# A hybrid HGRN2 and attention block: the second pair's accumulators evicted earlier in program order, the norm weight's row on GpSimd's queue

## The chip, the cores and the metric

The kernel runs on one core of one Trainium2 chip. The metric is the device time of one execution in microseconds (us); the time given for a kernel is the median of its runs. A profile is one further execution, recorded by the hardware.

The engines: PE (TensorE, matmuls; PEld are its weight loads), DVE (VectorE, elementwise), ACT (ScalarE, activations and copies), POOL (GpSimd) and SP (SyncE, which here only issues DMAs). Each works through its own queue in order. SPq, ACTq and POOLq are the DMAs that an engine issues.

## What is computed

One layer of a block with 256 rows of 2048 channels: an RMS norm, one wide input projection, an HGRN2 recurrence and a chunked attention on parts of it, a gated merge, an output projection, and an MLP with a squared ReLU. Cut to the part that the change lies in:

```python
u = rms_norm(h, norm_mix_w)
z = u @ w_in                                   # 2048 x 11264
hq, hf, hi, hg, aq, ak, av, gates = jnp.split(z, SPLIT_POINTS, axis=-1)
f = jax.nn.sigmoid(hf)
g = lb + (1.0 - lb) * f
log_g, kk = jnp.log(g), 1.0 - g
q = jax.nn.silu(hq) * (HG_DK ** -0.5)
o = hgrn2_scan(heads(q), heads(kk), heads(hi), heads(log_g))   # 8 heads of 128
y_a = rms_norm(o, hg_norm_w) * jax.nn.silu(hg)
y_b = chunk_band_attention(aq, ak, av, rel_bias)
merged = gate_a * (y_a @ w_branch_a) + gate_b * (y_b @ w_branch_b)
h = h + merged @ w_out
h = h + jnp.square(jax.nn.relu(rms_norm(h, norm_mlp_w) @ w_up)) @ w_down
out = rms_norm(h, norm_final_w)
```

## The kernel before

**Precision and matmuls.** Every large product is made of three: weights and activations are split into a high and a low part (`split`, L86: a cast on ACT to `wh`, L87, and a subtraction on DVE to `wl`, L88), and high x high, high x low and low x high are added up in one accumulator in PSUM. `weights` (L107) loads the weights by SP's queue, 1 MB at a time (L124), into three buffers `raw`, and splits each half into `wh` and `wl`, of which there are four buffers each.

**Accumulators.** `new_acc` (L146) takes one of two buffers (`ps_acc`). `gemm` (L149) makes a product with tokens on the partitions, `gemm_t` (L173, with `mm_t`, L180: matmuls at L185, L186 and L189) one with channels on the partitions. In the second form the two halves of an accumulator are added at the end by `add_parts` (L191): a copy on ACT (L193), then an addition on DVE (L194). Only after the addition is the buffer free for the accumulator after the next.

**The start.** The first loop (L219) makes hf and hq of pair 0 side by side while their inputs arrive. A pair is two of the eight HGRN2 heads: 256 channels of hf and 256 of hq. Then come, in program order, the constants (L248 to L285: lower bounds, masks, the row `hgw` of the norm weight spread over all partitions, L283), the eviction of pair 0 (L288 to L290: `f0`, `z0`), the product hf of pair 1 (`acc_f1`, L291), and the row norms: `squares` (L212) loads the rows of x by SP's queue, squares them on ACT, and `rows` (L236) turns 1/rms into a row over all partitions (`rstd_t`).

**The first half of the heads.** For g = 0 the loop at L485 calls `fq(0)` and `fq(1)`. `fq` (L474) evicts hf and hq of its pair, if need be makes them first, and calls `hf_pair` (L307: multiply by rstd, sigmoid, bounds, logarithm, scan) and `hq_pair` (L325: multiply by rstd, sigmoid, product). In `fq(1)` the product hf is there already (`acc_f1`), hq is made at L478. Then follow `v_chunk` (L338, the product hi, matmuls at L157 to L159), `hgrn_scores` of pair 0 (L359), `hg_chunk` (L347, the product hg, which reads `hgw` at L355), the scores of pair 1, and their values.

`hgrn_scores` makes the scores of a pair in eight small products `ps` (L366, L406) and a last one (L432), with two PSUM buffers (tag `sm`); DVE takes each out with a multiplication (L367) and masked copies (L368, L413) into `sd`. What it needs of ACT and DVE beforehand is exponentials and products (`el`, `er`, `rr`, `kl`, `qr`, L377 to L399).

**What sets the order.** Each engine's queue is written by a scheduler, which goes by the program's order and by priorities: `add_parts` and `split` stand in a `high_priority` block, so they are put ahead of elementwise work, but only as far as the place of their call lets them. Sigmoid, logarithm and exponential are different tables of ACT; a change of table is an instruction of its own (ACT_TABLE_LOAD).

Of the kernel before, what the change touches and what calls it, by code (L numbers as in the profile page):

```python
# [16 lines left out]
P = 128  # L17
T = 256
NM = T // P
D = 2048  # L20
KD = D // P
# [5 lines left out]
DK = 128  # L27
# [5 lines left out]
C_HQ, C_HF, C_AQ, C_AK, C_GA, C_GB = 0, HG, 2 * HG, 3 * HG, 4 * HG, 4 * HG + D  # L33
# [17 lines left out]
def tile_hybrid_block(  # L51
# [5 lines left out]
    nc = tc.nc  # L57
# [38 lines left out]
    def new_act(what):  # L96

        return apool.tile([P, 4, 2, T], F32R, name=f"act_{what}", tag="act")
# [47 lines left out]
    def new_acc(what):  # L146
        return ps_acc.tile([P, 2, NC], F32, name=f"acc_{what}", tag="acc")
# [25 lines left out]
    def gemm_t(rhs, w, n0, nkt, what):  # L173

        acc = new_acc(what)
        for a in weights(w, n0, nkt, T, what):
            mm_t(acc, rhs, nkt, *a)
        return acc

    def mm_t(acc, rhs, nkt, kt, wh, wl):  # L180
        r = rhs[kt // 4][:, kt % 4]
        for cb in range(2):
            c = slice(cb * P, (cb + 1) * P)
            if kt:
                nc.tensor.matmul(acc[:, cb, 0:T], wl[:, c], r[:, 0, :], start=False, stop=False)  # L185
            nc.tensor.matmul(acc[:, cb, :], wh[:, c], r.rearrange("p u t -> p (u t)"),  # L186
                             start=kt == 0, stop=kt == nkt - 1)
            if kt == 0:
                nc.tensor.matmul(acc[:, cb, 0:T], wl[:, c], r[:, 0, :], start=False, stop=False)  # L189

    def add_parts(dst, acc):  # L191
        with tc.high_priority(offset=2000):
            nc.scalar.copy(dst, acc[:, :, T:])  # L193
            nc.vector.tensor_tensor(dst, acc[:, :, 0:T], dst, op=ALU.add)  # L194
# [5 lines left out]
    def h2(what, bufs=10):  # L200
        return hp.tile([P, 2, T], F32, name=what, tag="h2", bufs=bufs)

    xT = [new_act(f"x{c}") for c in range(4)]
# [76 lines left out]
    nc.gpsimd.memset(reset, 1.0)  # L280
    nc.gpsimd.memset(reset.rearrange("p (c t) -> p c t", t=CH)[:, :, 0:1], 0.0)
    hgw = const.tile([P, DK], F32, name="hgw")
    nc.sync.dma_start(hgw, bass.AP(tensor=hg_norm_w.tensor, offset=hg_norm_w.offset, ap=[[0, P], [1, DK]]))  # L283
    c128 = const.tile([P, 2, 4], F32, name="c128")
    nc.gpsimd.memset(c128, 1.0)  # L285

# [1 line left out]
    f0, z0 = h2("f0"), h2("zq0")  # L288
    add_parts(f0, accs[0])
    add_parts(z0, accs[1])  # L290
    acc_f1 = gemm_t(xT, w_in_t, C_HF + T, KD, "hf1")  # L291
# [4 lines left out]
    rstd_t = rows(rstd, "rstd")  # L296
    rstd8_t = const.tile([P, T], F32, name="rstd8_t")
    nc.vector.tensor_scalar(rstd8_t, rstd_t, 0.125, None, op0=ALU.mult)


    def z_t(col, what, dst, factor, acc=None):
# [5 lines left out]
    def hf_pair(u, f):  # L307

        nc.vector.tensor_tensor(f, f, bc(rstd_t, 1, 2), op=ALU.mult)
        nc.scalar.activation(f, f, AF.Sigmoid)  # L310
        for h in range(2):
            hh = 2 * u + h
            nc.vector.tensor_scalar(f[:, h, :], f[:, h, :], omlb[:, hh:hh + 1], lb[:, hh:hh + 1],
                                    op0=ALU.mult, op1=ALU.add)
        kk = h2(f"kk{u}")
        nc.vector.tensor_scalar(kk, f, -1.0, 1.0, op0=ALU.mult, op1=ALU.add)
        nc.vector.tensor_scalar(f, f, LN_MIN, None, op0=ALU.max)
        lg = h2(f"lg{u}")
        nc.scalar.activation(lg, f, AF.Ln)
        b = h2(f"b{u}")  # L320
        nc.vector.tensor_tensor_scan(b.rearrange("p h t -> p (h t)"), reset,
                                     lg.rearrange("p h t -> p (h t)"), 0.0, ALU.mult, ALU.add)
        return f, kk, b

    def hq_pair(u, z, g):  # L325

        nc.vector.tensor_tensor(z, z, bc(rstd_t, 1, 2), op=ALU.mult)
        s = h2(f"sq{u}")
        nc.scalar.activation(s, z, AF.Sigmoid)
        q = hp.tile([P, 2, NM, 192], F32, name=f"q{u}", tag="q", bufs=2)  # L330
        half = lambda a: a.rearrange("p h (m t) -> p h m t", t=P)
        nc.vector.scalar_tensor_tensor(q[:, :, :, 0:P], half(z), DK ** -0.5, half(s), op0=ALU.mult, op1=ALU.mult)
        odd = lambda a: a.rearrange("p h m (j u) -> p h m j u", u=2)[:, :, :, :, 1]
        for h in range(2):
            nc.vector.tensor_tensor(q[:, h, :, P:], odd(q[:, :, :, 0:P])[:, h], odd(half(g))[:, h], op=ALU.mult)
        return q
# [135 lines left out]
        return finish  # L472

    def fq(u):  # L474
        if u:
            f, z = h2(f"f{u}"), h2(f"zq{u}")
            add_parts(f, acc_f1 if u == 1 else gemm_t(xT, w_in_t, C_HF + u * T, KD, f"hf{u}"))
            add_parts(z, gemm_t(xT, w_in_t, C_HQ + u * T, KD, f"hq{u}"))  # L478
        else:
            f, z = f0, z0  # L480
        g, kk, b = hf_pair(u, f)
        return kk, b, hq_pair(u, z, g)

    out0 = out1 = None
    for g in range(2):  # L485
        ya.append(new_act(f"ya{g}"))
        u = 2 * g
        a0 = fq(u)
        if out1:
            out1()  # L490
        a1 = fq(u + 1)
        vs = v_chunk(g)
        s0 = hgrn_scores(u, *a0)
        gws = hg_chunk(g)
        s1 = hgrn_scores(u + 1, *a1)
        out0 = hgrn_out(g, 0, s0, vs, gws)

        def out1(g=g, s1=s1, vs=vs, gws=gws, out0=out0):
            finish = hgrn_out(g, 2, s1, vs, gws)
            out0()  # L500
            finish()
# [152 lines left out]
    for qd in range(NQ):  # L654
# [12 lines left out]
        for n in range(4):  # L667
            end = last and n == 3
            acc = gemm(uT, w_down, n * NC, KD, f"dn{qd}{n}", tail=8 if end else 0, kt0=qd * KD)
            for m in range(NM):  # L670
# [11 lines left out]
                f = rstd3[:, m:m + 1]  # L682
# [53 lines left out]
```

## Time and profile before

| | |
|---|---|
| median of 3 runs | 1480.14 us (1478.12 to 1481.28) |
| the profiled execution | 1478.41 us, its span in the trace 1476.7 us |
| mean granted clock of PE | 0.995 |
| matmuls of the products hf, `acc_hf` L186, 128x512 | 128, 416 ns each as recorded |
| matmuls of the MLP, `acc_up` L186, 128x512 | 1024, 398 ns each as recorded |
| `hgw`, SP's issue and its landing | issued at 19.54 us, landing 7.0 us later |
| `gw` with `hgw` (L355) | first at 120.0 us, 4 times, median 675 ns |
| GpSimd's idle time before the row norm's power (L94) | 29.84 us, to 39.76 us |
| PE by stretches of 20 us, 0 to 80 us: granted clock | 1.00, 0.91, 1.00, 0.83 |

How to read the profile: a line of a timeline is a start, a duration, the engine, the line of the kernel, the operation, and what it writes and reads; in square brackets stands how long the engine was idle before it and what ended that. Matmuls are pipelined, so a recorded duration is longer than the distance to the next start. A clock of 1.00 is the full rate of TensorE. The chain is followed back from the last instruction to what released it.

### The profile page before, as it was taken

Reading aid. Unit: us, or ns where it says so; the run is one execution under the profiler, and the core shown is the slowest. Engines: PE = TensorE matmul, PEld = TensorE weight load, DVE = VectorE, ACT = ScalarE, POOL = GpSimd, SP = SyncE. Lnnn points to the kernel's source line nnn. Section 1 sums busy time; section 2 is a strip of 40 time slices with the busy share of each in tenths; the row PEclk is TensorE's granted clock in tenths of the full one; section 3 lists DMA queues with packets and bytes.
Section 4 is the critical chain, followed back from the end, with each engine's and each line's share of the span. In section 5 each row is a group of like instructions: output and inputs, shape, how many; then the busy total and the mean of one; then the engine's idle time right before and its main releaser. Section 6 shows DMA issues by size and latency. Waiting matters only on the chain.

```text
span 1476.7 us, 18045 instructions
## 1 busy us (share of the span) xinstructions
PE 1452.6 (98%) x7244; PEld 1222.5 (83%) x7244; DVE 881.1 (60%) x1180; ACT 713.2 (48%) x894; POOL 28.8 (2%) x85
## 2 busy tenths in 40 slices
PE   8899999999999999999999999999999999999997
PEld 7788888888788888888888888888888888888886
DVE  6797987565644444666565554566545665556554
ACT  6764844464544444344445544455434553355443
POOL 2000001010000000000000000000000000000000
PEclk9899999999999999999999999999999999999999
DMA  8444444545455555557545555555555555555552
GB/s 305 181 164 150 152 171 145 189 126 195 137 171 199 197 187 188 198 177 279 176 175 192 198 184 190 198 174 197 199 190 183 198 176 194 200 175 196 194 188 102
DMA packets 49045, 272.85 MB, mean 185 GB/s; under 512 B 5056, under 2 KB 5952, under 8 KB 23488
## 3 DMA queue, kind: packets, MB, share of 16 engines
q1 hardware_dynamic: 45744, 264.85, 51.5%
q10 hardware_dynamic: 2448, 4.74, 0.9%
q0 software_dynamic: 768, 2.10, 0.7%
q8 instruction: 57, 0.93, 0.2%
q14 instruction: 28, 0.23, 0.0%
HBM read 269.57 MB, written 2.10 MB: 184 GB/s over the span
## 4 chain that ended last, share of the span: by engine, by line
PE 93%; DVE 3%; DMA 1%; issue 1%; ACT 1%; POOL 0%; SPq 0%; POOLq 0%; ACTq 0%
PE acc_up L186 16%; PE acc_dn L157 8%; PE acc_dn L159 8%; PE acc_dn L158 8%; PE acc_up L185 8%; PE acc_ak L186 2%; PE acc_wo L158 2%; PE acc_wo L159 2%; PE acc_gb L159 2%; PE acc_gb L158 2%; PE acc_wo L157 2%; PE acc_gb L157 2%; PE acc_ga L159 2%; PE acc_ga L158 2%; PE acc_ga L157 2%; PE acc_aq L186 2%
## 5 line engine op out<-in xcount | busy, mean ns | idle before, releaser
L186 PE MATMUL acc_up<-act_h,wh_up 128*128 128x512 f32 x1024 | 359.2, 398 | 0.0
L185 PE MATMUL acc_up<-act_h,wl_up 128*128 128x256 f32 x960 | 269.7, 281 | 0.0
L88 DVE TENSOR_TENSOR wl_dn<-raw_dn,wh_dn 128x1024 fp32r<-128x1024 f32 x128 | 156.7, 1224 | 149.6 <-ACT wh_dn L87 149.6
L186 PEld LDWEIGHTS acc_up<-act_h,wh_up 128*128 128x128 f32 x1024 | 190.6, 188 | 44.4
L87 ACT CAST wh_dn<-raw_dn 128x1024 fp32r<-128x1024 f32 x128 | 135.1, 1055 | 186.3 <-PE acc_dn L159 172.2
L88 DVE TENSOR_TENSOR wl_up<-raw_up,wh_up 128x1024 fp32r<-128x1024 f32 x128 | 156.6, 1224 | 106.0 <-ACT wh_up L87 105.8
L158 PE MATMUL acc_dn<-wl_dn,act_u 128*128 128x512 f32 x512 | 199.2, 389 | 0.0
L159 PE MATMUL acc_dn<-wh_dn,act_u 128*128 128x512 f32 x512 | 199.2, 389 | 0.0
L157 PE MATMUL acc_dn<-wh_dn,act_u 128*128 128x512 f32 x512 | 199.1, 389 | 0.0
L87 ACT CAST wh_up<-raw_up 128x1024 fp32r<-128x1024 f32 x128 | 134.7, 1052 | 121.1 <-PE acc_up L186 93.0
L185 PEld LDWEIGHTS acc_up<-act_h,wl_up 128*128 128x128 f32 x960 | 181.3, 189 | 1.4
L159 PEld LDWEIGHTS acc_dn<-wh_dn,act_u 128*128 128x128 f32 x512 | 96.1, 188 | 20.1
L157 PEld LDWEIGHTS acc_dn<-wh_dn,act_u 128*128 128x128 f32 x512 | 96.1, 188 | 19.9 <-DVE h L672 0.2
L158 PEld LDWEIGHTS acc_dn<-wl_dn,act_u 128*128 128x128 f32 x512 | 96.1, 188 | 19.9
L88 DVE TENSOR_TENSOR wl_gb<-raw_gb,wh_gb 128x1024 fp32r<-128x1024 f32 x32 | 39.2, 1225 | 47.8 <-ACT wh_gb L87 47.8
L88 DVE TENSOR_TENSOR wl_ga<-raw_ga,wh_ga 128x1024 fp32r<-128x1024 f32 x32 | 39.2, 1225 | 43.4 <-ACT wh_ga L87 43.4
L88 DVE TENSOR_TENSOR wl_wo<-raw_wo,wh_wo 128x1024 fp32r<-128x1024 f32 x32 | 39.2, 1224 | 35.6 <-ACT wh_wo L87 35.6
L87 ACT CAST wh_wo<-raw_wo 128x1024 fp32r<-128x1024 f32 x32 | 33.8, 1055 | 49.3 <-PE acc_wo L159 38.3
L87 ACT CAST wh_gb<-raw_gb 128x1024 fp32r<-128x1024 f32 x32 | 33.8, 1057 | 48.6 <-PE acc_gb L159 41.9
L87 ACT CAST wh_ga<-raw_ga 128x1024 fp32r<-128x1024 f32 x32 | 33.8, 1055 | 45.3 <-PE acc_ga L159 38.6
L186 PE MATMUL acc_hf<-act_x,wh_hf 128*128 128x512 f32 x128 | 48.9, 416 | 2.7 <-DVE f L194 2.7
L159 PE MATMUL acc_ga<-wh_ga,act_x 128*128 128x512 f32 x128 | 50.5, 394 | 0.0
(305 smaller groups left out, 2752.4 us busy)
## 6 DMA issues: line engine op xcount, KB each, us to landing
raw_up<-in_w_up_dram SPq DMA_DIRECT2D x64, 1024.0 KB, 4.9
raw_dn<-in_w_down_dram SPq DMA_DIRECT2D x64, 1024.0 KB, 4.9
raw_ga<-in_w_in_t_dram SPq DMA_DIRECT2D x16, 1024.0 KB, 5.0
raw_gb<-in_w_in_t_dram SPq DMA_DIRECT2D x16, 1024.0 KB, 5.0
raw_wo<-in_w_out_dram SPq DMA_DIRECT2D x16, 1024.0 KB, 4.9
raw_hi<-in_w_in_n_dram SPq DMA_DIRECT2D x8, 1024.0 KB, 4.9
raw_hg<-in_w_in_n_dram SPq DMA_DIRECT2D x8, 1024.0 KB, 4.9
raw_aq<-in_w_in_t_dram SPq DMA_DIRECT2D x8, 1024.0 KB, 4.8
```

Of the source, the lines that this page charges most:

```text
L87: (copy or nc.scalar.copy)(hi, src)
L88: nc.vector.tensor_tensor(lo, src, hi.bitcast(F32), op=ALU.subtract)
L157: nc.tensor.matmul(part(m), h, wh, start=kt == 0, stop=False)
L158: nc.tensor.matmul(part(m), h, wl, start=False, stop=False)
L159: nc.tensor.matmul(part(m), lo, wh, start=False, stop=kt == nkt - 1)
L185: nc.tensor.matmul(acc[:, cb, 0:T], wl[:, c], r[:, 0, :], start=False, stop=False)
L186: nc.tensor.matmul(acc[:, cb, :], wh[:, c], r.rearrange("p u t -> p (u t)"), start=kt == 0, stop=kt == nkt - 1)
```

## The change

Two edits. `hgw` is loaded by GpSimd's queue. And the eviction of pair 1 (the copy and addition of hf, the product hq with its copy and addition) is written ahead of the definitions and calls of the elementwise work, right behind the row norms; `fq` then takes the evicted tiles for pairs 0 and 1.

```diff
     hgw = const.tile([P, DK], F32, name="hgw")
-    nc.sync.dma_start(hgw, bass.AP(tensor=hg_norm_w.tensor, offset=hg_norm_w.offset, ap=[[0, P], [1, DK]]))
+    nc.gpsimd.dma_start(hgw, bass.AP(tensor=hg_norm_w.tensor, offset=hg_norm_w.offset, ap=[[0, P], [1, DK]]))
...
     rstd8_t = const.tile([P, T], F32, name="rstd8_t")
     nc.vector.tensor_scalar(rstd8_t, rstd_t, 0.125, None, op0=ALU.mult)
+
+    f1, z1 = h2("f1"), h2("zq1")
+    add_parts(f1, acc_f1)
+    add_parts(z1, gemm_t(xT, w_in_t, C_HQ + T, KD, "hq1"))
...
     def fq(u):
-        if u:
+        if u == 0:
+            f, z = f0, z0
+        elif u == 1:
+            f, z = f1, z1
+        else:
             f, z = h2(f"f{u}"), h2(f"zq{u}")
-            add_parts(f, acc_f1 if u == 1 else gemm_t(xT, w_in_t, C_HF + u * T, KD, f"hf{u}"))
+            add_parts(f, gemm_t(xT, w_in_t, C_HF + u * T, KD, f"hf{u}"))
             add_parts(z, gemm_t(xT, w_in_t, C_HQ + u * T, KD, f"hq{u}"))
-        else:
-            f, z = f0, z0
         g, kk, b = hf_pair(u, f)
         return kk, b, hq_pair(u, z, g)
```

Lines of the kernel from L299 on move down by 4, those behind `fq` by 6 (L366 becomes L370, L406 becomes L410). The products, their sizes and their order on PE up to the scores are the same.

## The prediction

> **What bounds the kernel now.** I read the page first, then the waits of the first 300 us, then the timelines of PE, ACT and DVE around each wait, and last the windows with their clocks and the DMA issues. The page says that TensorE is the bound nearly everywhere:
>
> ```profile
> span 1476.7 us, 18045 instructions
> PE 1452.6 (98%) x7244; PEld 1222.5 (83%) x7244; DVE 881.1 (60%) x1180; ACT 713.2 (48%) x894; POOL 28.8 (2%) x85
> PE 93%; DVE 3%; DMA 1%; issue 1%; ACT 1%; POOL 0%; SPq 0%; POOLq 0%; ACTq 0%
> ```
>
> The reader is to see that an edit on DVE, ACT or a queue counts only where PE stands idle. The waits (engine, line, whom it waited for: total, times, longest) show two such places over 2 us; both are an accumulator waiting for `add_parts` (L194) to empty it:
>
> ```profile
> PE acc_hi L157 <- DVE f L194: 5.1, 1, 5.1
> PE acc_hf L186 <- DVE f L194: 2.7, 1, 2.7
> ```
>
> The large one, in the timelines of ACT, DVE and PE (start, duration):
>
> ```profile
> 59.01 1.28 ACT L329 ACT_TABLE_LOAD   x1
> 60.30 0.63 ACT L329 ACTIVATE sq<-zq 128x512 f32<-128x512 f32 x1
> 60.84 0.57 ACT L193 COPY f<-acc_hf 128x512 f32<-128x512 f32 x1
> ...
> 61.56 0.69 DVE L332 SCALAR_TENSOR_TENSOR q<-zq,sq 128x512 f32<-128x512 f32 x1
> 62.16 0.68 DVE L194 TENSOR_TENSOR f<-acc_hf,f 128x512 f32<-128x512 f32 x1
> ...
> 57.46 0.39 PE L186 MATMUL acc_hq<-act_x,wh_hq 128*128 128x512 f32 x1
> 62.99 0.76 PE L157 MATMUL acc_hi<-wh_hi,act_x 128*128 128x512 f32 x1 [5.14 <-DVE f L194]
> ```
>
> acc_hf of pair 1 has been complete since 46.2, but its copy and addition are queued behind pair 0's sigmoid, logarithm, scan and table loads, so the third accumulator (acc_hi), which takes its buffer, starts 5.1 us late. The clock then stays low for a while (windows: stretch; PE, PEld, DVE, ACT, POOL; granted clock, DMA):
>
> ```profile
> 30.00:35.00 5.00, 2.34 (x11) 1.78 (x11) 4.35 (x5) 4.08 (x7) 0.00 (x0) 0.94 1.01 423
> 35.00:40.00 5.00, 5.00 (x23) 4.30 (x22) 1.75 (x3) 3.99 (x5) 0.24 (x1) 0.72 1.01 426
> 60.00:65.00 5.00, 2.01 (x5) 1.66 (x6) 5.00 (x11) 4.94 (x8) 0.00 (x0) 0.67 0.54 182
> 65.00:70.00 5.00, 5.00 (x16) 3.92 (x15) 4.87 (x14) 4.32 (x6) 0.00 (x0) 0.65 0.07 28
> ```
>
> The small wait hangs on a DMA. The chain in order of time, and SP's issues:
>
> ```profile
> 20.85 8.19 DMA raw_hf<-in_w_in_t_dram
> ...
> 30.23 2.28 DVE wl_hf L88 x2
> 32.51 0.69 DVE f L194
> ...
> 18.35 1.15 SPq L124 DMA_DIRECT2D raw_hq<-in_w_in_t_dram  x1
> 19.54 1.21 SPq L283 DMA_DIRECT2D hgw<-in_hg_norm_w_dram  x1
> ```
>
> hgw's issue stands just ahead of the weights that this chain waits for.
>
> **The change, part by part.** *(a) The wait removed.* In the built order f1's copy moves on ACT from behind sq0 to behind the second cast of hq1, and its addition on DVE ahead of the rstd row; both are done about 1.2 us after PE ends hf1 at 46.2, so acc_hi's buffer is free by 47.5 and PE can go from hq1's last matmul (57.46+0.23 = 57.7) into acc_hi. The first pieces of hi's weights were split before that (by 52.6 in this trace). Gain 5.1. The clock adds to it: the first 13 matmuls of acc_hi take from 62.99 to 68.62 = 5.63 us, and 13 at the later spacing of 0.227 take 2.95. Gain 2.7; together 7.8.
>
> *(b) What is behind the moved instructions.* f1's copy now waits on ACT for PE's end of hf1, and the casts of hq1's second half (two of 1.05) queue behind it: they end near 48.8, DVE's halves near 50, PE wants them at 46.3+8x0.70 = 51.9 and later. Covered by 1.9 us. No instruction of arithmetic is added; ACT's table loads fall by two.
>
> *(c) The wait that comes instead.* PE now reaches pair 0's scores 7.8 us sooner; are ACT and DVE ready? Laid end to end in the new order, ACT from the copy of z1 (PE's end of hq1, 57.7) to its second cast of hg runs: a copy 0.46; seven casts of 1.05 = 7.35; seven table loads at 1.29 from start to start = 9.03 (Ln, Sigmoid and Exp of the two pairs take turns); activations of 0.54 (lg0, sq0, el, sq1), 0.65 (lg1), 0.41 (er), 0.24 (rr) = 3.46. Sum 20.3: 78.1. DVE then has, up to the masked copy (L368) that frees the first score buffer, three splits of 1.14, kl 0.61, qr 0.45, el 0.60, qr 0.33, kl 0.60, qr 0.20, sd 0.43, the masked copy 0.43 = 7.1: 85.2. PE gets there at 57.7 + 96x0.227 (acc_hi) + 1.16 (two score groups, 87.46 to 88.62) + 1.75 (seven matmuls of hg; the order has seven there, six before) = 82.4. New wait 2.8, where the trace has 0.17: cost 2.6. Bounds: 0 if nothing is late, and 7.8 if DVE reaches L368 no sooner than now (89.96). I take the worked 2.6.
>
> *(d) The clock after it.* Waits with a low clock behind them: 2.66 and 5.14 us. The longest without: 1.17, at 155.1. 2.8 is nearest to 2.66, so I count one stretch like that at 35 us, where five pairs of matmuls take 0.64 instead of 0.35 between 34.4 and 37.6, 1.4 us; with the windows it is 5x0.28+5x0.06 = 1.7. Cost 1.7; bounds 0 and 2.7. [...]
>
> *(e) hgw off SP's queue.* The cast of raw_hf waits for its landing (29.04), and everything to PE's start at 33.24 follows. The piece before hgw landed at 18.35+6.6 = 24.9, hgw at 19.54+7.0 = 26.5, and raw_hf 2.5 us later, which is what 1 MB takes there (the two halves of x land at 34.96 and 37.44). So hgw held the queue for up to 1.6 us; on SP itself it takes 1.3. On GpSimd's queue it is issued near 10 us, after the masks (GpSimd is then idle until 39.76) and is first read at 120. There DMA is at 0.98 to 0.99 of its time (5 to 15 us), and PE's margin over the splits is 1.2 us (hq's piece split by 16.48, used at 17.65), so 0.6 us or so of delay passes to the later pieces and PE does not see it. Gain between 0 and 1.6; I take 1.0. The wait of 2.66 becomes 1.7, nearer to 1.17 than to 2.66: its low clock, 1.4, is gone too. [...]
>
> Sum: -5.1-2.7+2.6+1.7-1.0-1.4 = -5.9 us. The profiled execution took 1478.4 (1476.7 span and 1.7 around it): 1472.5. It is 1.7 below the median of the runs, 1480.1, to which I apply the same sum: **1474.2**. From some 120 us on all engines' orders are the same, and no idle time of PE there is over 1.2 us.
>
> **Rivals.** *1: the whole wait moves to the scores.* DVE (18.1 of 20 us busy from 60 to 80) and ACT (19.2) are nearly full there; if they are no sooner at L368 than now, all 7.8 are given back and (e) alone stays: 1480.1-2.4 = 1477.7. Against it: ACT sheds two table loads, and after 84 it waits for PE for 1.7 and 4.4 us, so it has room. *2: no new wait.* If DVE and ACT overlap better than end to end: -7.8-2.4 = -10.2, 1469.9. Against: the 20.3 us on ACT have no idle time in them. *3: slower.* The norm row, now among the first weights, holds up all pieces by the 7.0 us that it took to land here. PE's margin of 1.2 then becomes a wait of 5.8 and a low clock of 1.7, (e) gains nothing: -3.5+7.5 = +4, 1484. It decides from a delay of 4.7 us on (3.5+1.2). For it: DMA is full there. Against: 64 KB, a quarter of one weight piece, and these land every 0.7 us. *Two halves of the forecast that may fall out differently*, within its 0.70: no low clock follows the new wait (0.3 of it; -7.6, 1472.5), and moving the norm row saves nothing on the weights' landing (0.2 of it; -3.5, 1476.6). [...] *That the scheduler undoes the edit* is out: the built order shows both moves.
>
> **How the numbers follow.** Forecast 0.70 (1471 to 1477), rival 1 0.14, rival 2 0.10, rival 3 0.06. Range 1469.5 to 1478.5: it takes in rivals 1 and 2 and the 1.7 us between the profiled execution and the median, and leaves out rival 3 and the ends of (c). 0.2% is 3 us, about what a measurement of this kernel tells from no change. Faster: the forecast, rival 2 and a little of rival 1, 0.80; same: most of rival 1, 0.14; slower 0.06.
>
> **What would show it.** (a): acc_hi starts within 0.3 us of hq1's last matmul, with the clock at 1.00 there. (c): a wait of PE of 2 to 4 us at ps (L410 after the change) near 82, ended by DVE's sd; none would speak for rival 2, over 6 for rival 1. (d): a clock near 0.7 in the 5 us after it. (e): raw_hf lands near 28 and the wait before acc_hf of pair 1 is below 2 us at full clock; a wait of PE before 30 us would speak for rival 3. I am wrong if the waits of the first 120 us together are not some 4 us smaller, or if anything after 120 us changes.

## The result, and the profile after

| | before | after |
|---|---|---|
| median of the runs | 1480.04 us (22 runs, 1475.99 to 1482.38) | 1474.46 us (22 runs, 1469.92 to 1483.7) |
| ratio of the runs | | 0.9963, 95% interval 0.9954 to 0.9973 |
| the profiled execution, and its span | 1478.41 us, 1476.7 us | 1475.12 us, 1473.3 us |

The change takes off 5.6 us by the medians, 0.37%. The two profiled executions are only 3.3 us apart; the section on the prediction comes back to that. The head of the page after, with the busy times and the chain by engine:

```profile
span 1473.3 us, 18041 instructions
PE 1450.8 (98%) x7244; PEld 1222.4 (83%) x7244; DVE 879.8 (60%) x1180; ACT 709.8 (48%) x892; POOL 29.9 (2%) x86
PE 92%; DVE 3%; DMA 2%; ACT 1%; issue 1%; POOL 0%; SPq 0%; POOLq 0%; ACTq 0%
```

PE is the bound as before, so the time is again read from the places where PE stands idle. The waits of PE from 15 to 300 us (total, times, longest):

```profile
PE ps L410 <- DVE sd L372: 3.3, 3, 2.9
PE acc_hf L186 <- DVE f L194: 3.0, 1, 3.0
PE tpo L473 <- DVE ms L93: 1.2, 1, 1.2
...
PE acc_hq L185 <- DVE wl_hq L88: 0.8, 1, 0.8
```

The 5.1 us at acc_hi are gone. A wait of 2.9 us at pair 0's block scores (L410) has come, and the first wait, at acc_hf of pair 1, is not shorter but 3.0 us where it was 2.7. The timelines of PE and DVE around the first two places:

```profile
58.20 0.39 PE L186 MATMUL acc_hq<-act_x,wh_hq 128*128 128x512 f32 x1
58.44 0.39 PE L157 MATMUL acc_hi<-wh_hi,act_x 128*128 128x512 f32 x1
...
82.90 0.39 PE L157 MATMUL acc_hg<-wh_hg,act_x 128*128 128x512 f32 x1
86.18 1.62 PE L410 MATMUL ps<-qr,kl 128*128 128x192 f32 x4 [2.90 <-DVE sd L372]
...
84.14 0.41 DVE L371 TENSOR_TENSOR sd<-ps,ident 128x256 f32<-128x256 f32 x1
84.48 1.21 DVE L88 TENSOR_TENSOR wl_hg<-raw_hg,wh_hg 128x1024 fp32r<-128x1024 f32 x1
85.61 0.43 DVE L372 COPY_PREDICATED sd<-mask,ps 128x128 f32<-128x128 int32 x1
```

acc_hi follows hq1's last matmul at the usual distance, and the block scores start when the masked copy L372 has emptied the first score buffer. The windows (stretch; PE, PEld, DVE, ACT, POOL; clock, DMA):

```profile
30.00:35.00 5.00, 2.01 (x10) 1.46 (x9) 3.67 (x4) 4.75 (x6) 0.00 (x0) 0.95 1.01 423
35.00:40.00 5.00, 5.00 (x24) 4.36 (x23) 2.33 (x4) 4.16 (x5) 0.06 (x1) 0.71 1.02 429
60.00:65.00 5.00, 5.00 (x23) 4.14 (x23) 4.63 (x5) 4.94 (x7) 0.00 (x0) 1.00 0.45 141
...
85.00:90.00 5.00, 3.82 (x13) 3.62 (x14) 3.86 (x13) 1.05 (x2) 0.00 (x0) 0.66 0.59 210
```

From 60 to 65 us the clock is now 1.00 (0.67 before); it is low again behind the new wait (0.66), and still low behind the first one (0.71). Last the chain in order of time (start, duration), and GpSimd's issue of the norm row in its timeline:

```profile
20.57 9.57 DMA raw_hf<-in_w_in_t_dram
...
31.33 1.47 DVE wl_hf L88 x2
32.79 0.81 issue
33.61 0.69 DVE f L194
```

```profile
10.38 0.72 POOL L283 DMA_DIRECT2D hgw<-in_hg_norm_w_dram  x1
```

hf1's first weights landed at 30.15, against 29.04 in the trace of before, although the row no longer stands ahead of them.

### The profile page after: what moved, and what is told of

Same layout as the page of the kernel before. It is cut to its first block, busy times and chain, and to the rows that moved or that the text cites. A ratio compares the mean times of both kernels' runs of the same rounds, so it can differ in the third digit from the quotient of the medians.

```text
span 1473.3 us, 18041 instructions
## 1 busy us (share of the span) xinstructions
PE 1450.8 (98%) x7244; PEld 1222.4 (83%) x7244; DVE 879.8 (60%) x1180; ACT 709.8 (48%) x892; POOL 29.9 (2%) x86
## 4 chain that ended last, share of the span: by engine, by line
PE 92%; DVE 3%; DMA 2%; ACT 1%; issue 1%; POOL 0%; SPq 0%; POOLq 0%; ACTq 0%
PE acc_up L186 16%; PE acc_dn L159 8%; PE acc_dn L158 8%; PE acc_dn L157 8%; PE acc_up L185 8%; PE acc_ak L186 2%; PE acc_wo L157 2%; PE acc_wo L158 2%; PE acc_wo L159 2%; PE acc_gb L158 2%; PE acc_gb L157 2%; PE acc_gb L159 2%; PE acc_ga L159 2%; PE acc_ga L158 2%; PE acc_ga L157 2%; PE acc_aq L186 2%
```

## The experiments

Times are medians; ratios are to the kernel before on the same chip. "The whole change" is the changed kernel. There were three groups of runs (e0 to e3; g2 to g4 and h1; e4, h6, f9 and j2), in which the kernel before took 1480.02, 1479.60 and 1479.21 us, so medians of different groups can be compared to about 1 us only.

**The two edits apart.** In `e1_evict_only` L283 says `nc.sync` again; `e2_row_only` is the kernel before with only that line changed; in `e3_row_late` SP issues the row, behind the loads of x:

```diff
-    nc.gpsimd.dma_start(hgw, bass.AP(tensor=hg_norm_w.tensor, offset=hg_norm_w.offset, ap=[[0, P], [1, DK]]))
...
     for m in range(NM):
         squares(m)
+    nc.sync.dma_start(hgw, bass.AP(tensor=hg_norm_w.tensor, offset=hg_norm_w.offset, ap=[[0, P], [1, DK]]))
```

> The changed kernel once more, beside the next three, so that differences of about 1 us can be read on one chip. By the first measurement 5.6 us below the kernel before. In its first trace the first weight piece of hf1 landed 1.1 us later (30.15 against 29.04) and hq1's last matmul began 0.74 us later (58.20 against 57.46) than before the change. If that comes from the norm row on GpSimd's queue, it is here again (landing near 30.1, 58.2); if it was chance of one execution, it lies elsewhere, near 29.0 and 57.5.

> The early eviction alone; the norm row stays on SP's queue. Theory S (the prediction's step e: the row holds SP's queue for 1.0 us and the first wait's low clock hangs on it): 2.4 us slower than the whole change, so about 3.2 us below before. Theory M (the row is only moved, it costs the same on either queue): the same as the whole change within 0.5 us. Theory C (the row on GpSimd's queue delays the weights that are landing from 10 to 18 us): 0.7 to 1.5 us faster than the whole change, with raw_hf of hf1 landing near 29.0 and no wait of PE near 20 us. In all three the wait for acc_hi is gone and one of 2.5 to 3.5 us stands at the scores.

> The norm row on GpSimd's queue alone; eviction order as before. Theory S: 2.4 us below before. Theory M: as before within 0.5 us. Theory C: 0.7 to 1.5 us above before, with the new wait of some 0.8 us near 20 us. The waits of 5.1 us before acc_hi and of 0.2 us at the scores are there again.

> The whole change, but the norm row is issued by SP behind the two loads of x, so it stands neither among the first weights nor ahead of hf1's. Theory S: SP's queue is free by 1.0 to 1.6 us for raw_hf of hf1 (landing 27.5 to 28), the first wait is below 2 us at full clock, and the time equals the whole change or is up to 1 us below it. Theory M: as the whole change within 0.5 us. Theory C: 0.7 to 1.5 us faster than the whole change, and as fast as or faster than the eviction alone.

| | median | ratio, 95% interval | mean clock over the runs | hf1's weights landed, first wait |
|---|---|---|---|---|
| before | 1480.02 (21 runs) | 1 | 0.9944 | 29.04, 2.66 |
| whole change again | 1474.65 (5) | 0.9963 (0.9949 to 0.9977) | 0.9964 | 30.97, 2.95 |
| eviction alone | 1476.75 (11) | 0.9975 (0.9966 to 0.9985) | 0.9955 | 29.22, 3.30 |
| row alone | 1477.47 (11) | 0.9987 (0.9978 to 0.9996) | 0.9954 | 29.39, 2.84 |
| row issued late | 1474.42 (5) | 0.9963 (0.9949 to 0.9976) | 0.9956 | 29.76, 2.90 |

By the times theory S holds: the eviction is worth 3.3 us, the row 2.6 alone and 2.1 on top (the 2.1 is a difference of two medians whose intervals overlap), and the sum of the two alone, 5.8, is about the whole. Theory M is out for the row alone, since its interval excludes 1, and theory C has the sign wrong. Theory S's picture in the trace is not there, though: no first wait is below 2 us, and a half rate follows each.

Part of the row's gain shows in the clock. Every run has its mean granted clock; row alone has 0.0009 more than before (0.99536 and 0.99443), which is 0.0009 x 1477 = 1.4 us of lost time less. Of all 53 runs of before in the three groups, 6 had 0.996; of the 11 with the row alone, 6 had. One stretch of half rate of 3.41 us (85.71 to 89.13 us in the trace of the whole change) counts as half of its length, 1.7 us, or 0.0012 of the mean, so it looks as if moving the row spares such a stretch in some of the executions. That is not shown: each kernel has one trace, and half rate follows the first wait in all of these. The mean also takes in the end of the program, 3.8 to 6.7 us at half rate behind the last matmul in the fourteen traces (5.3 before, 5.2 with the whole change), which costs nothing and moves the mean of a single run by up to 0.001.

**An accumulator of its own for hf1.** The two score buffers are empty until 80 us; here they take hf1's accumulation, so that it needn't wait for f0's eviction, and hi takes hq0's buffer instead of hf1's. `add_parts` then copies and adds in halves (its lines, and those of `mm_t`, are left out here).

```diff
-    acc_f1 = gemm_t(xT, w_in_t, C_HF + T, KD, "hf1")
+    acc_f1 = [ps_sm.tile([P, NC], F32, name=f"acc_hf1_{cb}", tag="sm") for cb in range(2)]
+    for w1 in weights(w_in_t, C_HF + T, KD, T, "hf1"):
+        mm_t(acc_f1, xT, KD, *w1)
```

> The whole change, and the accumulator of hf1 in the two score buffers, which are empty then, in place of acc's second round: PE need not wait for f0's eviction. In the traces that eviction stands on ACT behind both casts of hf1's first piece (30.25 to 32.15) and on DVE behind both splits (31.33 to 33.61), and PE starts at 34.34. Theory A (the first wait is one for a buffer): PE starts when the first cast is done, near 31.3, pauses 0.5 to 1 us for the split, no low clock near 35: 3 to 4 us below the whole change, about 1471, with the wait at the scores as before, 2.5 to 3 us. Theory L (the landing of hf1's weights sets it): the wait stays above 2.4 us, and the time is that of the whole change within 0.7 us.

> The kernel before (eviction late, norm row on SP's queue) with the accumulator of hf1 in the two score buffers. acc_hi then takes hq0's buffer, which is free from 36 us on. Theory A (the early eviction was worth only the wait for that buffer): no wait at acc_hi, and within 1 us of the next kernel, which has the early eviction; 6 to 9 us below before. Theory O (the order on ACT and DVE counts by itself, or the late copy of f1 holds up something else): 2 to 5 us slower than the next kernel.

> As the first of these (early eviction, own accumulator for hf1), but the norm row on SP's queue. Theory W (the row's 1.8 us come through the first wait and its low clock): with that wait gone the row is worth nothing, so within 0.7 us of the first. Theory Q (the row costs SP's queue or the DMA engines its time whatever PE waits for): 1.5 to 2.5 us slower than the first.

1470.77 us (7 runs, ratio 0.9957, 0.9938 to 0.9976) with the whole change; 1471.01 (7 runs, 0.9953, 0.9935 to 0.9970) on the kernel before; 1471.83 (5 runs, 0.9948, 0.9936 to 0.9960) with the early eviction and the row on SP. Theory A holds in both places. The waits of PE in the kernel before with the own accumulator, and its timelines of PE and ACT at acc_hi:

```profile
PE ps L415 <- DVE sd L377: 3.4, 3, 3.0
...
PE acc_hf L187 <- ACT wh_hf L87: 1.0, 1, 1.0
PE acc_hf L190 <- DVE wl_hf L88: 0.8, 1, 0.8
```

```profile
56.55 0.39 PE L187 MATMUL acc_hq<-act_x,wh_hq 128*128 128x512 f32 x1
56.78 0.39 PE L157 MATMUL acc_hi<-wh_hi,act_x 128*128 128x512 f32 x1
...
60.00 0.63 ACT L196 COPY f<-acc_hf 128x256 f32<-128x256 f32 x2
```

f1's copy still stands at 60.00, behind sq0, but nobody waits for it: acc_hi starts at 56.78 right behind hq1, and the wait has gone on to the scores (3.0 us), just as with the early eviction. The times show nothing that the early eviction is worth beyond the buffer it frees: with the row on SP's queue in both, the kernel without it took 1471.01 us and the one with it 1471.83, with intervals some 5 and 4 us wide. (The first two of the three kernels have wide intervals because single runs took 1477.0 to 1480.4 us, at mean clocks of 0.990 to 0.993.) The first wait ends with the first cast now, no longer with f0's addition. Whether the row is worth anything once that wait is short stays open: medians 1.1 us apart, between theory W's 0.7 and theory Q's 1.5, and the ratios, with wide intervals, lean the other way.

**The wait at the scores.** In `h1_more_score_buffers` the two groups of the first block level go into the transpose buffers:

```diff
-                ps = ps_sm.tile([P, NM, 192], F32, name=f"ps{n}_{B}{h}", tag="sm")
+                pool, tag = (ps_tp, "tp") if n == 0 and i == 0 else (ps_sm, "sm")
+                ps = pool.tile([P, NM, 192], F32, name=f"ps{n}_{B}{h}", tag=tag)
```

In `e4_pair1_later` pair 1's elementwise work is called behind pair 0's scores; `h6_split_wait` is both of these:

```diff
-        a1 = fq(u + 1)
+        a1 = fq(u + 1) if g else None
...
         s0 = hgrn_scores(u, *a0)
+        a1 = a1 or fq(u + 1)
```

> The whole change, and the first two groups of block scores of pair 0 in the two idle transpose buffers, so that they do not wait for the masked copy into sd. Theory D (the chain of ACT and DVE up to that copy sets the time, as in the prediction's step c): the wait only moves two groups on, to the next level's scores, 2.3 to 3.2 us long, and the time is that of the whole change within 0.7 us. Theory P (two score buffers are too few): no wait over 0.5 us and no low clock near 87, 3.5 to 4.5 us below the whole change.

> The whole change, with pair 1's elementwise work (from f1, z1 to kk, b, q) behind pair 0's scores in program order. Theory D (what stands ahead of the masked copy on ACT and DVE sets the wait): the masked copy that frees the first score buffer comes 1.5 to 3 us sooner; the built order has two matmuls of hg ahead of the block scores in place of seven, so the wait stays 2 to 3 us and the time is 0.3 to 1.5 us below the whole change. Theory F (the chain through f0, z0 and pair 0's own work sets it, whatever pair 1 does): the copy comes when it did, the wait is over 4 us, and the time is up to 1 us above.

> As the one before, and the first two groups of block scores in the transpose buffers; these two groups then stand between the two waits of PE. Theory H (half rate follows when more than about half of a window of 3.4 us is idle, counted in windows that lie on a fixed grid from one half rate to the next): the wait falls into two of 1 to 2 us with work between, the half rate after it appears in some executions and not in others, and the median is 1 to 2.5 us below the whole change. Theory S (the half rate follows each single wait of over about 2 us): two waits below 2 us and no half rate near 85 in any. Theory T (it follows the sum of idleness, wherever it lies): half rate there as ever, and at most 1 us below the whole change.

h1: 1473.54 us (5 runs, 0.9961, 0.9949 to 0.9973). Its timelines of PE and DVE:

```profile
80.46 1.46 PE L411 MATMUL ps<-qr,kl 128*128 128x192 f32 x8
81.62 0.53 PE L157 MATMUL acc_hg<-wh_hg,act_x 128*128 128x512 f32 x1
85.12 1.62 PE L411 MATMUL ps<-qr,kl 128*128 128x192 f32 x4 [2.96 <-DVE sd L372]
...
82.87 0.28 DVE L403 TENSOR_TENSOR qr<-qr,rr 128x128 f32<-128x128 f32 x1
84.54 0.43 DVE L372 COPY_PREDICATED sd<-mask,ps 128x128 f32<-128x128 int32 x1
```

The first level runs at once, and the next one waits 2.96 us for the same masked copy: theory D, the wait only moves two groups on. It is still a wait for a buffer, though. PE is idle from 82.16, and the last input of that next level (qr, L403) is done at 83.15; so 1.0 us of the wait is for inputs, and the other 2.0 for the copy that stands behind them in DVE's queue. Whether buffers for every level would save those 2.0 us was not tried. e4: 1473.4 us (5 runs, 0.9961, 0.9949 to 0.9973); PE waits 2.38 us, ended by the same copy. Counted from the start of acc_hi the block scores begin at 83.60 - 57.50 = 26.1 us, against 86.18 - 58.44 = 27.7 with the whole change: the copy comes 1.6 us sooner when pair 1's work stands behind it, as theory D says. Five of hg's seven matmuls (5 x 0.23 = 1.1 us) go behind in exchange, so little is left of it. h6: 1473.65 us (8 runs, 0.9965, 0.9952 to 0.9979). The wait is split, 1.59 and 0.61 us, but the gain that theory H gave for it isn't there in the median; two of the eight runs had a mean clock of 0.999 and took 1470.6, the others 1472.3 and more. Theory S is out: there are two waits below 2 us, and a half rate follows. Theory T fits the median too (0.8 us below the whole change); what decides between T and H are the windows below.

**The clock behind a wait.** `f9_fill_wait` has nine matmuls of constants on PE ahead of the block scores; nothing reads them:

```diff
+    def fill(i, n):
+        tp = ps_tp.tile([P, 4, P], F32, name=f"tp_fill{i}", tag="tp")
+        for _ in range(n):
+            nc.tensor.matmul(tp[:, 0, :], warm, warm, start=True, stop=True)
...
+            if n == 0 and i == 0:
+                fill(1, 9)
             for h in range(2):
                 ps = ps_sm.tile([P, NM, 192], F32, name=f"ps{n}_{B}{h}", tag="sm")
```

> The whole change, with nine matmuls of constants (128x128, 0.43 us each in the warm-up, 3.9 us) on PE between pair 0's first scores and its block scores; their result is not used. In the built order the seven matmuls of hg that stood there (1.6 us) come behind. Theory I (the half rate follows PE's idleness, as in the prediction's step d): PE's wait at the scores is below 1.3 us, no half rate follows near 87, so +1.6 for the seven matmuls and -1.7 for the clock: the time of the whole change within 0.7 us, with a mean clock higher by 0.001. Theory N (the half rate there comes from something else, such as the time since the last one): it is there again, and the time is 1.3 to 1.9 us above the whole change.

1476.08 us (12 runs, 0.9991, 0.9975 to 1.0007), 1.6 above the whole change (2.2 to 2.5 if each is counted from the kernel before in its own group of runs), so the time is about what theory N gave. But the trace doesn't bear out its reason: the nine matmuls took 2.17 us and not 3.9 (0.24 each; the 0.43 came from the warm-up at the program's start, where the same matmuls took nearly twice as long), a wait of 2.51 us stayed, and no half rate followed it in this execution. In others it may have: the runs with a mean clock of 0.998 took 1473.6 and 1473.8 us, those with 0.995 took 1475.9 to 1476.5. What PE did ahead of it is seen in windows cut at multiples of 3.413 us from the trace's first half rate; 3.413 us is how long that first half rate lasted by the granted clock in the traces of before (34.40 to 37.81) and of the whole change (34.51 to 37.93). The columns are stretch; PE busy; clock, DMA. The whole change:

```profile
82.30:85.71 3.41, 0.99 (x5) 1.00 0.59 247
85.71:89.13 3.42, 2.95 (x10) 0.50 0.67 223
89.13:92.54 3.41, 3.41 (x19) 1.00 0.20 84
```

The filled wait:

```profile
80.71:84.12 3.41, 2.00 (x18) 1.00 0.71 286
84.12:87.53 3.41, 2.27 (x11) 1.00 0.50 151
```

The kernel before and the early eviction with the own accumulator (g3, then g4), at hf1's start:

```profile
29.80:33.21 3.41, 1.60 (x8) 1.00 0.99 406
33.21:36.62 3.41, 3.41 (x13) 0.50 1.02 430
```

```profile
28.46:31.87 3.41, 2.22 (x13) 1.00 0.98 360
31.87:35.29 3.42, 2.35 (x12) 1.00 0.98 410
```

In each of these windows the clock is 1.00 or 0.50 and nothing between. In the whole change PE is idle for 2.42 of 3.41 us (71%), and the next window is at half rate. The filled wait of 2.51 us lies across a border and leaves 1.41 and 1.14 us idle (41% and 33%), with full rate in both windows and in the next. g4's two waits, 2.26 us together, are cut into 1.19 and 1.07 us (35% and 31%): full rate; g3's 1.81 us lie in one window (53%): half rate. So in these traces the half rate goes neither with the length of a wait (2.51 us without it in the filled kernel, 2.10 with it in h6) nor with the sum of several (2.26 without, 1.81 with), but with how much of one window was idle.

**Both gains together.** `j2_combined` is h6 with the accumulator of its own.

> The one before with the own accumulator of hf1: what the runs so far showed to help, together. First wait below 1.5 us without half rate (-3.5 against the whole change, as in the kernel with the own accumulator alone, 1470.8), and the wait at the scores split in two (-1 to -2): 1469 to 1470, 9.5 to 11 us below before. If the two gains do not add, because ACT and DVE set the scores however early PE is there, 1470.8 as without the split.

1469.28 us (6 runs, 1468.83 to 1475.36; ratio 0.9940, 0.9928 to 0.9953): faster than either kernel. The gain is the forecast one of 9.5 to 11 us (1479.21 - 1469.28 = 9.9 on that chip; 8.9 by the ratio, in which the one run of 1475.36 counts). Its PE:

```profile
30.32 0.47 PE L187 MATMUL acc_hf<-act_x,wh_hf 128*128 128x512 f32 x1
31.55 0.38 PE L190 MATMUL acc_hf<-act_x,wl_hf 128*128 128x256 f32 x1 [0.77 <-DVE wl_hf L88]
...
80.16 0.89 PE L420 MATMUL ps<-qr,kl 128*128 128x192 f32 x4 [1.57 <-DVE sd L381]
...
81.88 1.59 PE L420 MATMUL ps<-qr,kl 128*128 128x192 f32 x4 [0.60 <-DVE sd L381]
```

hf1 starts without a wait and pauses 0.77 us for its split; nothing of the first half rate is left. At the scores there is one: from 81.88 us four score matmuls take 1.14 us up to the next start (83.02), where the four from 80.16 took 0.59. That the split wait adds anything to the own accumulator alone (1470.77) is not shown: the two were measured in different groups of runs, their intervals overlap, and h6 alone gained nothing clear.

## Why the prediction was right, and where its reasons were not

The forecast of 1474.2 us was met (1474.46), in part by luck, as (e) shows. One of the signs that it named for its being wrong did come: the waits of PE in the first 120 us were to be some 4 us smaller together, and in the two traces they are 9.83 us before and 8.30 after, 1.5 us smaller, since the first wait grew by 0.3 where it was to shrink by 1.0, and one of 0.83 us came at 21 us. The other half of what separates these two executions is one window of half rate less, two in place of three (1.7 us). Behind 120 us nothing changed, as forecast: from the first matmul into `po` to the last one of the program PE took 1336.1 us in both. The steps, with what the runs showed:

**(a) The wait removed: right, in mechanism and size.** From hq1's last matmul to the first scores PE took 87.46 - 57.46 = 30.0 us before and 80.22 - 58.20 = 22.0 after: 8.0 us, predicted 7.8. The own accumulator on the kernel before shows that the freed buffer is all of it: there the same stretch takes 78.57 - 56.55 = 22.0 us.

**(b) What queues behind the moved copy: right.** PE has no wait over 0.1 us in hf1 and hq1, whose casts could have suffered, and acc_hi starts 0.24 us behind its predecessor.

**(c) The new wait: right.** 2.90 us, predicted 2.8 (57.7 + 20.3 is 78.0 and not 78.1, so the sum gives 2.7); its end is DVE's L372, as predicted. h1 shows that two more score buffers don't shorten it, and e4 shows that pair 1's work, which the sum on ACT and DVE counted, does stand ahead of the copy. Rival 1 (over 6 us) and rival 2 (none) are both out.

**(d) The low clock behind it: it came; its price was somewhat too high, and the wait's length was the wrong thing to go by.** The whole change takes 151.77 - 86.18 = 65.6 us from the block scores to the next wait of 1.2 us; the filled kernel takes 151.13 - 85.21 = 65.9 with seven more matmuls (1.6 us) and no half rate. So the low clock cost 65.6 - (65.9 - 1.6) = 1.3 us in this execution, predicted 1.7. The prediction went by the length of the wait, 2.8 us being nearest to 2.66. In the windows above the half rate goes with the idle share of one window: 71% ahead of it at this wait and 53% in g3, against 41% and 33% without it in the filled kernel. So in another execution the same wait may have none behind it; that is an estimate from these windows.

Terms (a), (c) and (d) gave -3.5; the eviction alone measured -3.3.

**(e) The row off SP's queue: the size came out, the path to it did not.** The steps that failed are "raw_hf lands near 28" and "the wait of 2.66 becomes 1.7 ... its low clock, 1.4, is gone too". In the nine traces with the row on GpSimd's queue hf1's weights landed between 28.29 and 30.97, median 29.19; in the four with the row on SP's, ahead of them, between 29.04 and 30.99, median 29.84. That is 0.65 us earlier in the middle, where 1.0 was predicted, inside a spread of 2.7. What did come sooner in every trace is SP's issue of these weights: at 19.10 to 20.57 us in the nine, at 20.75 to 21.16 in the four, 0.96 us in the middle; but from issue to landing they took 8.2 to 10.8 us, and most of the lead is lost in that. The late landing of the first trace (30.15) and of its repeat (30.97) is not what the move brings, since the other seven landed by 29.39. The first wait, with the shared accumulator, was 2.10 to 3.06 us in the seven traces with the row on GpSimd's queue and 2.66 and 3.30 in the two with it on SP's; half rate followed in all.

The runs still give the row 2.1 to 2.6 us where 2.4 was predicted, with a higher mean clock, which points to a low window spared in some executions. That the size came out is luck as far as the reasons given go. The half of the forecast in which moving the row saves nothing (1476.6) is not borne out by the times; they show a gain. A late issue on SP did as well (1474.42) as GpSimd's queue (1474.65), so the gain does not need another issuer. What made the gain beyond the 0.65 us was not settled. The traces can't settle it: the two with the shared accumulator and the row ahead on SP's queue are of executions 1.6 and 2.2 us below the medians of their kernels, those of the whole change and of the row alone 0.7 to 2.8 us above.

Rival 3 (the row holds up the first weights) is out as a loss. A trace of it is there: PE waited 0.83 and 0.63 us near 20 us in the two traces of the whole change, and in none of the other traces by more than 0.4; what is late there is hq0's weights.

**Profile and medians.** By the first trace of the whole change the row seemed to have gained nothing; eleven runs each of the parts said otherwise. One execution shows which wait ends what, and its clock; differences of 1 or 2 us need the runs.

## What to carry to other kernels

Where a matmul waits for a buffer to be emptied, look for an idle buffer before reordering the work of the engines that empty it: on the kernel before, two idle score buffers alone gave 8.6 us by the medians (1479.60 to 1471.01; 7.0 by the ratio, 4.4 to 9.6), where the reordering and the moved row together gave 5.6. When a wait goes, work out at once which engine's queue PE meets next: more than half of the wait removed here came back 28 us later. And a wait's low clock was not to be read off its length here: 1.05 and 0.76 us inside one window of 3.41 us (g3) had one stretch of half rate behind them, as the 2.90 us of the whole change had, and 1.50 and 0.76 us shared between two windows (g4) had none.

## What the runs showed of the hardware that was not expected

The half rate came in stretches of 3.41 us, or of twice or three times that. Ahead of the last 20 us the trace of before has it from 34.40 to 37.81 and from 61.71 to 68.53 us, that of the whole change from 34.51 to 37.93 and from 85.71 to 89.13: 3.41 us, and once 6.83. Their starts lie 27.31 and 51.20 us apart, 8 and 15 times 3.413.

Cut at 3.413 us from the first half rate, and without the first 5 and the last 20 us, these two traces have 844 windows at full rate that are followed by another. In 840 of them PE was idle for 36% or less, and the next was at full rate; in the other four it was idle for 66%, 100%, 71% and 88%, and the next was at half rate. The windows of the other traces that were cut so fit in: full rate followed 31% to 41% (g4 and the filled kernel), half rate 53% (g3), 60% (h6), 63% (the whole change again) and 64% (row issued late). Of the windows at half rate, those with 14% idle or less were followed by full rate, and those with 22% (row issued late), 23% (the whole change again) and 38% (before, from 61.71 us) by another half one. In the last 20 us of the two traces, where PE ends its work, half rate follows a window that is idle throughout; but with the row issued late one that is 56% idle, from 1464.24 us, was followed by full rate. So these are shares that were seen, not a sharp number; what a window idle for 42% to 52% is followed by is not shown, nor whether these shares are the same in another program.

Where the borders lie against the program differs from trace to trace (first half rate between 32.9 and 34.5 us where the first wait brought one), and the runs of one kernel spread with the clock: the whole change took 1470.7 us with a mean clock of 0.998, 1472.4 with 0.997 and 1474.9 with 0.996.

One case is outside this altogether. In the profiled execution of the combined kernel (1475.36 us, the others at most 1469.78) a half rate of three windows (10.24 us) begins at 385.69 behind a window 39% idle, and stays through two in which PE was never idle:

```profile
382.28:385.69 3.41, 2.07 (x16) 1.57 (x14) 1.20 (x5) 1.79 (x6) 0.69 (x2) 1.00 0.83 315
385.69:389.11 3.42, 3.42 (x10) 2.02 (x10) 1.77 (x9) 1.31 (x4) 0.84 (x3) 0.50 0.31 62
389.11:392.52 3.41, 3.41 (x14) 2.66 (x13) 2.68 (x7) 1.81 (x7) 0.69 (x2) 0.50 0.16 31
392.52:395.93 3.41, 3.41 (x12) 2.93 (x13) 0.86 (x4) 0.00 (x0) 0.15 (x1) 0.50 0.13 24
```

There the score matmuls of the attention use 64 of 128 rows (L539 and L540, 64*128 in the trace). Why it stayed low is open; other kernels had single runs with a mean clock of 0.989 to 0.993 whose place was not traced.
